# Two layers of a hybrid encoder on one core: the sixth product's own weights at byte 320 modulo 512, and the hand-over work of VectorE and ScalarE in another order

## The chip, the cores and the metric

The kernel runs on one core of a Trainium2 chip. The metric is device time of one execution in microseconds (us), lower is better. The engines are TensorE (PE in the profile; PEld its weight loads), VectorE (DVE), ScalarE (ACT), GpSimd (POOL) and SyncE (SP), which here only issues transfers. SBUF is the on-chip memory with 128 partitions, PSUM the eight banks that TensorE writes.

## The reference

Two layers over 512 tokens of width 1024, float32. Each layer:

```python
h = h + 0.5 * post(SwiGLU(pre(h)))        # w_gu: 1024 x 5632, w_down: 2816 x 1024
u = pre(h); proj = u @ w_in               # 1024 x 6912: q, k, v of three attentions, gates
m = sum_i gate_i * (branch_i @ W_branch_i)
h = h + post(m @ W_out)
h = h + 0.5 * post(SwiGLU(pre(h)))
```

`pre` and `post` are RMS norms with gains; a gate is the sigmoid of its part of `proj` plus `b_gate`. The weights of a layer are used once in a run, so they are streamed from HBM.

## The kernel before

**Split operands.** Every float32 operand of a matmul is split into a high part (rounded to float32r by a ScalarE copy) and a low part (VectorE subtracts the high part). A product is three matmuls: high by high, high by low, low by high. So each weight tile costs one ScalarE and one VectorE operation before TensorE may use it. `ensure` does this for plain streamed weights (L209, L210). Their tiles, the `r13` and `w12` below, and four tiles of the down projection (`part`, L645) share the tag `wp` with four buffers.

**The feed-forward, first half.** A few of the 22 column blocks of the gate and up weights (4, or 6 in the first) are plain products. For each of the other 16 to 18 blocks, 70 in all four feed-forwards, the 2x2 product of weight quadrants and halves of the tokens is made by seven products with sums and differences of the quadrants, in place of eight. Each is a call of `product`: twelve matmuls of 256 columns, all at L856. In a block g they stand in TensorE's queue as p1, p7, p3 of block g-1, p6, p4, p2, p5. Their weights are `h1` (p1 and p4), `h13` (p7 and p5), `h24` (p3 and p6) and their low parts, from a pool of the phase, whose tiles lie at byte 320 modulo 512; p2 alone uses `w12` (tag `wp`, at 0 modulo 512), the sixth product's own weights. Their moving operands lie at 0, but that of p5 (`t1`) at 320. p2 adds into a bank of tag `at` that ScalarE has seeded with p1's sum (L895); the others use tag `mm`. In the trace, w12 is written at L728 (ACT) and L731 (DVE), and carries the name `w`.

**The feed-forward, second half.** The down projection is seven products over 8 and one part over 6 blocks of rows, in 34 units: 4 each of kinds 1, 7, then 3 of n2, 4 of 6, 4 of 4, 3 of n1, and 4 each of 2, 5 and 3. A unit is twelve or more matmuls of 512 columns (L1096). `prep` makes the split weights of a unit (`wh` at L972 on ScalarE, `wl` at L973 on VectorE); `preps(n)` makes all up to unit n, and `then` says which load from HBM follows which preparation. `t3(c)` makes one half of the moving operand of kind 7: a difference (L1005) and its split (L999, L1000). Work beside a unit hangs on it through `job`. From the end of the blocks on, the order on TensorE, ScalarE and VectorE is that of the code (`ordered`, a manual schedule); elsewhere a scheduler places instructions.

**The hand-over.** `Handover` takes the finished sums of a sub-layer to the next operand, for four blocks of 128 tokens (`tb`): squares with their sums (L449, `junk`), the gain (L465), a root (L458), its reciprocal (L462), the addition to the residual (L474), the next norm (L487), transposes on TensorE (`turn`, L522), split copies of the transposed operand (`operand`, L531 and L532) and plain ones (`plain`, L537). `late` runs the chain for one block and calls what it is given in `between`: the first after the gain, the second between the root and the reciprocal. In a feed-forward `first_rows` does it for blocks 0 and 1 beside kind 5, and L1258 adds the last sum before kind 3 may write its bank. The function Sqrt needs a table that ScalarE loads when the first instruction asks for it (ACT_TABLE_LOAD).

**The mixer.** Three attentions, gates (tanh with half the bias, L1558) and branch products, in the order of a table; then `m @ W_out` with the hand-over beside it, in `ordered`.

Of the kernel before, what the change touches and what calls it, by code (L numbers as in the profile page):

```python
# [10 lines left out]
F32 = mybir.dt.float32  # L11
# [5 lines left out]
P = 128  # L17
# [98 lines left out]
def encoder_kernel(ctx: ExitStack, tc: tile.TileContext, order, xT, wts, cols, rows, rpb, consts, tables, out):  # L116
# [6 lines left out]
    dr = ctx.enter_context(tc.tile_pool(name="dr", bufs=1, space=bass.MemoryType.DRAM))  # L123
    phase = [None]

    BUFS = {"X": 6, "n": 2, "wr": 3, "wp": 4}
    ABUFS = {"f": {"t": 4, "x": 10}, "m": {"t": 5, "h": 4, "rr": 2, "tx": 5, "st": 16, "g": 10, "s": 2, "pt": 4}}
    PBUFS = {"mm": 4, "at": 3, "o": 1}

# [11 lines left out]
    def nm(s):  # L141
        serial[0] += 1
        return f"{s}{serial[0]}"
# [19 lines left out]
    cons = cp.tile([P, CONSTW], F32, tag="cons", name="cons")  # L163
    colt = cp.tile([P, NCOLS], F32, tag="colt", name="colt")
    ones = cp.tile([P, P], F32, tag="ones", name="ones")
    half = cp.tile([P, NCOLS], F32, tag="half", name="half")
    epst = cp.tile([P, 1], F32, tag="eps", name="eps")
    sink = cp.tile([P, L, 8], F32, tag="sink", name="sink")
    misc = cp.tile([P, 2 * L + 1], F32, tag="misc", name="misc")
# [9 lines left out]


    HB = WB // 2
    stream = {"raw": [], "ready": [], "made": 0, "held": {}, "limit": 0, "stop": NTILES * 2, "later": [], "pace": 1, "eng": nc.scalar, "beside": []}

    def wpart(name, dt=F32R):
        t = sb.tile([P, 2, HB, P], dt, tag="wp", name=nm(name), bufs=BUFS["wp"])
        return t[:, 0], t[:, 1]

    def holder(tag):
# [97 lines left out]
    def first_loads(hT):  # L286
        def load(hs, *bs):
            for b in bs:
                nc.sync.dma_start(hT[:, b, hs], xT[b * P : (b + 1) * P, hs])

        load(HALVES[0], 0)
        fetch(2, nc.sync)
        load(HALVES[0], 1, 2)
        fetch(1, nc.sync)
        load(HALVES[0], 3, 4, 5)
        fetch(1, nc.sync)
        load(HALVES[0], 6, 7)
        load(HALVES[1], *range(KD))
        nc.sync.dma_start(cons, consts)
        warm = bank("o")  # L300
        for _ in range(WARM):
            PE.matmul(warm[:, :P], ones, ones, start=True, stop=True)
        V.tensor_scalar(out=half, in0=colt, scalar1=0.5, scalar2=None, op0=ALU.mult)

    def mm3(acc, w, x, start, stop):
        if len(x[0].shape) == 3:
# [72 lines left out]
    def announce(first, spare):  # L379

        assert len(order) % HB == 0
        at = len(order) // HB
        stream["limit"] = at + len(first) * KD // HB
        held = range(at + BUFS["wp"], stream["limit"])
        stream["held"] = dict(zip(held, spare))
        assert len(held) <= len(spare)

# [17 lines left out]
    class Operand:  # L405


        def __init__(self, raw):
            form = (P, 2, KD // 2, T // 2)

            def tiles(tag, dt, name):
                return [sb.tile(list(form), dt, tag=tag, name=nm(name), bufs=BUFS[tag]) for _ in range(2)]

            self.hi, self.lo = [], []
            for _ in range(2):
                for part in (self.hi, self.lo):
                    part.append(sb.tile(list(form), F32R, tag="X", name=nm("X"), bufs=BUFS["X"]))
            self.raw = tiles("n", F32, "n") if raw else None
            h = KD // 2
            self.blocks = [(self.hi[k // h][:, :, k % h, :], self.lo[k // h][:, :, k % h, :]) for k in range(KD)]  # L420

    class Handover:

# [145 lines left out]
    def ffn(l, which, X, accs):  # L569
# [71 lines left out]
        def settle(u):  # L641

            for parts in (PH, PL):
                if u < 2:
                    t = sb.tile([P, 2, T], F32R, tag="wp", name=nm("part"), bufs=BUFS["wp"])  # L645
# [78 lines left out]
            V.tensor_tensor(out=raws[g][1][:, 1], in0=W[g]["r13"][:, 1], in1=raws[g][0][:, 0], op=ALU.add)  # L724

        def high12(g):
            W[g]["h12"], W[g]["l12"] = wpart("w12")
            A.activation(W[g]["h12"], raws[g][1][:, 0], AF.Copy)  # L728

        def low12(g):  # L730
# [351 lines left out]
        p3(count - 1)  # L1082
        silu1(count - 1)
        gated(count - 1)
        t3(1)

        a, c, e, d = [], [], [], []
# [323 lines left out]
    def mixer(l, op, first):  # L1411
# [142 lines left out]
        def gates(n, *ms):  # L1554
            for m in ms:
                pg = dense1(w, l, GL + n * KD + m, X)
                t = gate0[m // 4][:, m % 4, :] if n == 0 else big("g", name="gate")
                A.activation(t, pg, AF.Tanh, scale=0.5, bias=col("b_gate", l, n * KD + m, half))  # L1558
                gate[n, m] = t

        def combine(n, key, *ms):
# [197 lines left out]
```

## Time and profile before

| | us |
|---|---|
| median of 3 runs | 2418.13 (2414.67 to 2418.2) |
| the profiled execution | 2413.36 |
| its span | 2411.6 |
| TensorE busy | 2379.9 |
| VectorE busy | 1782.5 |
| ScalarE busy | 1342.9 |
| mean granted TensorE clock | 0.999 |

The span runs from the first to the last instruction of the profiled execution; 1.8 us of that execution lie around it. A row of the timeline gives start, length, engine, line, operation, output and inputs, shapes and, in brackets, how long the engine stood idle before it and what ended that. Ends of matmuls are modelled (0.28 us for 256 columns, 0.39 for 512) and overlap the next ones, so the pace of TensorE is read from the distances between starts. Lines of the feed-forward stand four times in a run, and those of the mixer twice.

### The profile page before, as it was taken

How to read it: one execution, taken by the hardware profiler on the slowest of the kernel's cores; microseconds unless marked ns; L12 is line 12 of the kernel's file. 1: busy time of each engine (PE TensorE's matmuls, PEld its weight loads, DVE VectorE, ACT ScalarE, POOL GpSimd, SP SyncE). 2: the span in 40 equal slices, each digit the busy share in tenths (PEclk: the TensorE clock that was granted, in tenths of full speed). 3: DMA queues.
4: the chain of work that ended last, by engine and by line, in shares of the span. 5: the costliest groups of instructions: out<-in, count | busy, mean ns of one | idle time of the engine just before them, and what ended most of it. 6: DMA issues, size and time to landing. Idle time of an engine off the chain costs nothing. (4 is left out here: it accounts for less than half of the span.)

```text
span 2411.6 us, 37743 instructions
## 1 busy us (share of the span) xinstructions
PE 2379.9 (99%) x14266; PEld 2084.2 (86%) x14266; DVE 1782.5 (74%) x2959; ACT 1342.9 (56%) x2487; POOL 193.2 (8%) x192
## 2 busy tenths in 40 slices
PE   9999999999999999999999999999999999999998
PEld 8999888888777889998899998878887778899987
DVE  8887975757667467888878878767676764788786
ACT  6555655646555365655655555556565554556563
POOL 0111000000111100110001110000011111011100
PEclk9999999999999999999999999999999999999999
DMA  5566536435443334664525565374354333246642
GB/s 172 159 169 184 172 128 179 127 105 153 118 123 97 114 105 134 170 159 164 168 89 165 159 174 192 112 184 115 115 149 124 114 96 122 97 148 168 187 144 90
DMA packets 119190, 340.46 MB, mean 141 GB/s; under 512 B 15968, under 2 KB 22752, under 8 KB 118496
## 3 DMA queue, kind: packets, MB, share of 16 engines
q1 hardware_dynamic: 91344, 224.72, 30.0%
q10 hardware_dynamic: 22032, 79.78, 11.0%
q0 software_dynamic: 5632, 33.56, 6.9%
q8 instruction: 112, 1.84, 0.3%
q14 instruction: 70, 0.57, 0.1%
HBM read 285.03 MB, written 48.23 MB: 138 GB/s over the span
## 5 line engine op out<-in xcount | busy, mean ns | idle before, releaser
L308 PE MATMUL mm<-X,w 128*128 128x512 f32 (+1 forms) x1044 | 396.0, 379 | 2.6 <-ACT w L209 1.2
L309 PE MATMUL mm<-X,w 128*128 128x512 f32 (+1 forms) x1044 | 396.4, 380 | 0.8 <-DVE X L532 0.7
L310 PE MATMUL mm<-X,w 128*128 128x512 f32 (+1 forms) x1044 | 396.1, 380 | 0.0
L210 DVE TENSOR_TENSOR w<-wr,w 128x512 fp32r<-128x512 f32 x360 | 255.1, 714 | 170.7 <-ACT w L209 168.5
L209 ACT ACTIVATE w<-wr 128x512 fp32r<-128x512 f32 x360 | 223.5, 627 | 224.7 <-PE mm L310 178.5
L856 PE MATMUL mm<-ht,l 128*128 128x256 f32 x1120 | 311.1, 278 | 0.0
L856 PE MATMUL mm<-ht,h 128*128 128x256 f32 x1120 | 311.1, 278 | 0.0
L856 PE MATMUL mm<-lt,h 128*128 128x256 f32 x1120 | 310.9, 278 | 0.0
L308 PEld LDWEIGHTS mm<-X,w 128*128 128x128 f32 x1044 | 196.8, 189 | 35.0 <-ACT X L531 1.4
L309 PEld LDWEIGHTS mm<-X,w 128*128 128x128 f32 x1044 | 196.9, 189 | 32.8 <-DVE X L532 1.1
L310 PEld LDWEIGHTS mm<-X,w 128*128 128x128 f32 x1044 | 196.6, 188 | 30.8
L856 PEld LDWEIGHTS mm<-ht,h 128*128 128x128 f32 x1120 | 210.8, 188 | 0.0
L856 PEld LDWEIGHTS mm<-ht,l 128*128 128x128 f32 x1120 | 210.8, 188 | 0.0
L856 PEld LDWEIGHTS mm<-lt,h 128*128 128x128 f32 x1120 | 210.8, 188 | 0.0
L1096 PE MATMUL mm<-wh,f 128*128 128x512 f32 x640 | 201.3, 393 | 0.0
L856 PE MATMUL mm<-X,h 128*128 128x256 f32 x1120 | 199.1, 277 | 0.0
L856 PEld LDWEIGHTS mm<-X,h 128*128 128x128 f32 x1120 | 170.1, 188 | 0.5 <-DVE v L910 0.2
L856 PE MATMUL mm<-X,l 128*128 128x256 f32 x560 | 154.9, 277 | 0.0
L1096 PEld LDWEIGHTS mm<-wh,f 128*128 128x128 f32 x640 | 120.3, 188 | 26.3
L713 DVE TENSOR_TENSOR l<-wr,h 128x1024 fp32r<-128x1024 f32 x70 | 85.7, 1224 | 70.9 <-PE mm L856 70.9
L1096 PE MATMUL mm<-wl,f 128*128 128x512 f32 x320 | 125.4, 392 | 3.1 <-DVE wl L973 3.1
L334 ACT ACTIVATE hi<-at 128x256 fp32r<-128x256 f32 (+2 forms) x168 | 73.9, 453 | 73.0 <-PE at L1389 33.6
(370 smaller groups left out, 5431.9 us busy)
## 6 DMA issues: line engine op xcount, KB each, us to landing
wr<-in_wts_dram SPq DMA_DIRECT2D x223, 512.0 KB, 4.9
wr<-in_wts_dram ACTq DMA_DIRECT2D x152, 512.0 KB, 3.7
sum<-in_wts_dram POOLq DMA_DIRECT2D x64, 512.0 KB, 5.4
st<-hi SPq DMA_DIRECT2D x84, 128.0 KB, 2.3
st<-lo SPq DMA_DIRECT2D x84, 128.0 KB, 3.2
ap<-in_wts_dram SPq DMA_DIRECT2D x20, 512.0 KB, 6.5
a<-kept SPq DMA_DIRECT2D x32, 256.0 KB, 6.2
ap<-sum SPq DMA_DIRECT2D x16, 512.0 KB, 3.3
```

The costliest lines, as they stand in the source:

```text
L209: A.activation(hi, raw, AF.Copy)
L210: V.tensor_tensor(out=lo, in0=raw, in1=f(hi), op=ALU.subtract)
L308: PE.matmul(acc, w[0], x[0], start=start, stop=False)
L309: PE.matmul(acc, w[0], x[1], start=False, stop=False)
L310: PE.matmul(acc, w[1], x[0], start=False, stop=stop)
L334: A.activation(hi, src, AF.Copy)
L713: V.tensor_tensor(out=W[g]["l1"], in0=raws[g][0], in1=f(W[g]["h1"]), op=ALU.subtract)
L856: PE.matmul(acc, ws[i], xs[j], start=start and k == n == 0, stop=stop and k == HK - 1 and n == 2, skip_group_check=True,)
L1096: PE.matmul(acc, x[i], w[j], start=start and n == 0, stop=stop and n == 2, skip_group_check=True)
```

## The change

```diff
-    BUFS = {"X": 6, "n": 2, "wr": 3, "wp": 4}
+    BUFS = {"X": 6, "n": 2, "wr": 3, "wp": 2, "wq": 2}
+    WP = BUFS["wp"] + BUFS["wq"]
+    SKEW = 80
...
-    half = cp.tile([P, NCOLS], F32, tag="half", name="half")
+    cp.tile([P, 24], F32, tag="room", name="room")
...
+    def skewed(name, at, dt=F32R):
+
+        t = sb.tile([P, 2 * T + 128], dt, tag="wq", name=nm(name), bufs=BUFS["wq"])
+        return t[:, at : at + 2 * T]
 
     def wpart(name, dt=F32R):
-        t = sb.tile([P, 2, HB, P], dt, tag="wp", name=nm(name), bufs=BUFS["wp"])
+        stream["turn"] = not stream["turn"]
+        if stream["turn"]:
+            t = sb.tile([P, 2, HB, P], dt, tag="wp", name=nm(name), bufs=BUFS["wp"])
+        else:
+            t = skewed(name, 0, dt).rearrange("p (a b c) -> p a b c", a=2, b=HB)
         return t[:, 0], t[:, 1]
...
-        V.tensor_scalar(out=half, in0=colt, scalar1=0.5, scalar2=None, op0=ALU.mult)
+        for l in range(L):
+            at = COLS["b_gate", l]
+            own = colt[:, at : at + 24]
+            V.tensor_scalar(out=own, in0=own, scalar1=0.5, scalar2=None, op0=ALU.mult)
...
+    def root_table():
+        A.activation(dummy, ones[:, 0:1], AF.Sqrt)
...
         def high12(g):
-            W[g]["h12"], W[g]["l12"] = wpart("w12")
+            t = skewed("w12", SKEW).rearrange("p (a b c) -> p a b c", a=2, b=HB)
+            W[g]["h12"], W[g]["l12"] = t[:, 0], t[:, 1]
             A.activation(W[g]["h12"], raws[g][1][:, 0], AF.Copy)
...
         p3(count - 1)
         silu1(count - 1)
         gated(count - 1)
+        preps(4)
         t3(1)
...
-        job("2", 0, move_plain)
+        job("2", 0, move_plain, root_table)
...
         region = ordered()
         region.__enter__()
         stream["eng"] = nc.sync
+        root_table()
         for k in range(KD):
...
-        H.late(1, 1, last[1], lambda: H.operand(0), lambda: weights(1))
+        H.late(1, 1, last[1], lambda: H.operand(0), lambda: None)
+        weights(1)
         H.plain(0)
```

The four buffers of tag `wp` become two of `wp` and two of `wq`; a tile of `wq` is 512 bytes longer. Streamed weights take the two kinds in turn, `r13` takes `wp` alone, `w12` takes `wq` alone and starts 80 floats, 320 bytes, into it. The down projection's `part` tiles use both kinds from their start. The tile `half` goes; the gate biases are halved in place, and a small unused tile keeps the residue modulo 512 of what lies behind it. Other tiles move by 512 bytes or by none.

Three places of the order change. At the start of a down projection, on VectorE, where `wl` are the low parts of units 2, 3 and on, and `lt` and `f` are the second half of `t3`. Before:

```order
L1000 TENSOR_TENSOR f_2817<-ht_2814,f_2816 128x1024
L924 TENSOR_TENSOR a_2520<-t_2832,v_2747 128x2x256
L1005 TENSOR_TENSOR lt_2858<-a_2520,a_1048 128x1024
L1000 TENSOR_TENSOR f_2817<-lt_2858,f_2816 128x1024
L973 TENSOR_TENSOR wl_2863<-wr_2712,wh_2862 128x1024
L973 TENSOR_TENSOR wl_2869<-wr_2765,wh_2868 128x1024
L973 TENSOR_TENSOR wl_2875<-ht_2836,wh_2874 128x1024
```

Of the change:

```order
L1022 TENSOR_TENSOR f_2818<-ht_2815,f_2817 128x1024
L946 TENSOR_TENSOR a_2521<-t_2833,v_2748 128x2x256
L995 TENSOR_TENSOR wl_2860<-wr_2713,wh_2859 128x1024
L995 TENSOR_TENSOR wl_2866<-wr_2766,wh_2865 128x1024
L1027 TENSOR_TENSOR lt_2871<-a_2521,a_1049 128x1024
L1022 TENSOR_TENSOR f_2818<-lt_2871,f_2817 128x1024
L995 TENSOR_TENSOR wl_2876<-ht_2837,wh_2875 128x1024
```

Two low parts stand ahead of the difference and its split now; ScalarE's high parts move in the same way.

Beside kinds 2 and 5 of the first feed-forward, on ScalarE, where `share` are copies of the plain part's sums and `misc` is the output of `root_table`. Before:

```order
L1154 ACTIVATE share_3440<-o_3335 128x512
L972 ACTIVATE wh_3444<-ap_3026 128x1024
L972 ACTIVATE wh_3461<-ap_3026 128x1024
L209 ACTIVATE w_3465<-wr_3275 128x512
L972 ACTIVATE wh_3480<-ap_3026 128x1024
L209 ACTIVATE w_3484<-wr_3275 128x512
L972 ACTIVATE wh_3499<-ap_3026 128x1024
L209 ACTIVATE w_3503<-wr_3311 128x512
L209 ACTIVATE w_3506<-wr_3311 128x512
L449 ACTIVATE junk_3521,sh_3522<-at_884 128x512
L196 DMA wr_3945<-in_wts_dram 128x1024
L458 ACT_TABLE_LOAD
```

Of the change:

```order
L1177 ACTIVATE share_3441<-o_3336 128x512
L438 ACT_TABLE_LOAD
L438 ACTIVATE misc<-ones 128x1
L994 ACTIVATE wh_3446<-ap_3027 128x1024
L438 ACTIVATE misc<-ones 128x1
L994 ACTIVATE wh_3463<-ap_3027 128x1024
L220 ACTIVATE w_3467<-wr_3276 128x512
L994 ACTIVATE wh_3482<-ap_3027 128x1024
L220 ACTIVATE w_3486<-wr_3276 128x512
L994 ACTIVATE wh_3501<-ap_3027 128x1024
L220 ACTIVATE w_3505<-wr_3312 128x512
```

The load stands right behind the copies. The second `misc` is the mixer's call of `root_table`: it depends on nothing, and stands in the feed-forward before the mixer. In the mixer the load stays where it was, ahead of the first root, and the number of table loads stays at 30.

In the mixer's hand-over, on VectorE, where `w` is a streamed weight's low part and `y` the normed rows of token block 1. Before:

```order
L454 TENSOR_SCALAR sh_8874<-sh_8874 128x1
L210 TENSOR_TENSOR w_8883<-wr_8818,w_8882 128x512
L462 RECIPROCAL sh_8878<-sh_8878 128x1
L487 SCALAR_TENSOR_TENSOR y_8523<-h_8519,sh_8878,gain_8529 128x512
L487 SCALAR_TENSOR_TENSOR y_8524<-h_8519,sh_8878,gain_8529 128x512
L465 TENSOR_TENSOR y_8526<-mm_8718,gain_8529 128x512
```

Of the change:

```order
L472 TENSOR_SCALAR sh_8877<-sh_8877 128x1
L480 RECIPROCAL sh_8881<-sh_8881 128x1
L505 SCALAR_TENSOR_TENSOR y_8525<-h_8521,sh_8881,gain_8531 128x512
L505 SCALAR_TENSOR_TENSOR y_8526<-h_8521,sh_8881,gain_8531 128x512
L221 TENSOR_TENSOR w_8892<-wr_8821,w_8891 128x512
L483 TENSOR_TENSOR y_8528<-mm_8721,gain_8531 128x512
```

The low part stands behind the two norms now. TensorE's order and those of GpSimd and SP are unchanged.

More of the change, by code (lines that the diff above doesn't have):

```diff
@@ L181, in encoder_kernel @@
     HB = WB // 2
-    stream = {"raw": [], "ready": [], "made": 0, "held": {}, "limit": 0, "stop": NTILES * 2, "later": [], "pace": 1, "eng": nc.scalar, "beside": []}
+    stream = {"raw": [], "ready": [], "made": 0, "held": {}, "limit": 0, "stop": NTILES * 2, "later": [], "pace": 1, "eng": nc.scalar, "beside": [], "turn": False}
+    def skewed(name, at, dt=F32R):
+        t = sb.tile([P, 2 * T + 128], dt, tag="wq", name=nm(name), bufs=BUFS["wq"])
+        return t[:, at : at + 2 * T]
     def wpart(name, dt=F32R):
-        t = sb.tile([P, 2, HB, P], dt, tag="wp", name=nm(name), bufs=BUFS["wp"])
+        stream["turn"] = not stream["turn"]
[3 more added lines that the diff above has]
+            t = skewed(name, 0, dt).rearrange("p (a b c) -> p a b c", a=2, b=HB)
         return t[:, 0], t[:, 1]
@@ L383, in announce @@
         stream["limit"] = at + len(first) * KD // HB
-        held = range(at + BUFS["wp"], stream["limit"])
+        held = range(at + WP, stream["limit"])
         stream["held"] = dict(zip(held, spare))
@@ L644, in settle @@
                 if u < 2:
-                    t = sb.tile([P, 2, T], F32R, tag="wp", name=nm("part"), bufs=BUFS["wp"])
+                    if u == 0:
+                        t = sb.tile([P, 2, T], F32R, tag="wp", name=nm("part"), bufs=BUFS["wp"])
+                    else:
+                        t = skewed("part", 0).rearrange("p (a b) -> p a b", a=2)
                     parts.append([t[:, 0, :], t[:, 1, :]])
@@ L1557, in gates @@
                 t = gate0[m // 4][:, m % 4, :] if n == 0 else big("g", name="gate")
-                A.activation(t, pg, AF.Tanh, scale=0.5, bias=col("b_gate", l, n * KD + m, half))
+                A.activation(t, pg, AF.Tanh, scale=0.5, bias=col("b_gate", l, n * KD + m))
                 gate[n, m] = t
```

## The prediction

> **What bounds the kernel now.** I read the shares of the engines first, then the windows inside a feed-forward stage, then who waited for whom on TensorE.
>
> ```profile
> PE 2379.9 (99%) x14266; PEld 2084.2 (86%) x14266; DVE 1782.5 (74%) x2959; ACT 1342.9 (56%) x2487; POOL 193.2 (8%) x192
> ...
> 2190.00:2199.69 9.69, 9.69 (x87) 9.69 (x86) 1.00 0.69 166
> ...
> PE mm L1096 <- DVE ht L1258: 3.5, 3, 1.2
> PE mm L1096 <- DVE wl L973: 3.1, 4, 0.8
> ...
> PE at L522 <- DVE y L487: 1.7, 2, 0.8
> ...
> PE mm L308 <- ACT X L531: 0.6, 2, 0.3
> ```
>
> TensorE is busy for 99% of the span. The window (its length, then PE and PEld busy, granted clock, DMA share, GB/s) is one block of a feed-forward's gate and up weights: 9.69 us without a hole at clock 1.00. So only two things shorten the run: matmuls that issue closer together, and the few stalls in the last four rows (total, times, longest, in us). The change touches both.
>
> **Part A: the sixth product's weights.** The `product` calls of a block run on TensorE as p1, p7, p3 (of the block before), p6, p4, p2, p5, twelve matmuls of 256 columns each.
>
> ```profile
> L856 PE MATMUL at<-X,w 128*128 128x256 f32 x840 | 111.9, 283 | 0.0
> ...
> 2218.90 0.28 PE L856 MATMUL mm<-ht,h 128*128 128x256 f32 x1
> ...
> 2220.33 0.40 PE L856 MATMUL mm<-X,h 128*128 128x256 f32 x2
> ...
> 2227.15 1.60 PE L856 MATMUL at<-X,w 128*128 128x256 f32 x12
> 2228.58 0.28 PE L856 MATMUL mm<-ht,h 128*128 128x256 f32 x1
> ```
>
> Only p2 writes an `at` bank, so the first row is p2: 840 matmuls, 70 blocks. In one block p5 runs from 2218.90 to 2220.33 (1.43 us), then p1, p7, p3, p6 and p4 to 2227.15 (6.82 us, 1.364 each), then p2 to 2228.58 (1.43). Two products take 0.066 us more than the other five, with the same shapes. What sets these two apart is where their operands lie modulo 512 bytes, in the program's placement: p2 has weights and moving operand both at 0, p5 both at 320; the other five have weights at 320 and moving operands at 0. The change puts p2's weights at 320. Of all matmuls in the program, these 840 alone change their pair of residues.
>
> The other side is bounded by the opening products of a stage, also 256 wide:
>
> ```profile
> 12.24 0.28 PE L308 MATMUL mm<-X,w 128*128 128x256 f32 x1
> ...
> 13.67 0.28 PE L308 MATMUL at<-X,ht 128*128 128x256 f32 x1
> ...
> 16.50 0.28 PE L308 MATMUL mm<-X,w 128*128 128x256 f32 x1
> ```
>
> Twelve with both operands at 0 take 1.43 us (119 ns each); 24 with weights at 320 (`ht`, `lt`) take 2.83 us (118 ns). There the residue buys 1 ns; these change bank every three matmuls, p2 stays in one. If p2 behaved like them, 840 x 1 ns = 0.8 us would come. No row shows a residue pair of this kind that loses. I take p2 as nearest to p4, same line, same shape and one bank: 70 x 0.066 = **4.6 us**, ends 0.8 and 5.0.
>
> The Trainium skill, "TensorE: Matmul & The Clock Gate", section "Step-by-step: what each phase is for", says that TensorE has two independent SBUF read ports, so that loading the next weights takes no read bandwidth from the running matmul. By that rule the place of the weights would not matter and part A would be 0. The 1.43 against 1.364 us above speaks against it here.
>
> p2's tile comes from a pool of two now, where w12 could take any of four buffers. ScalarE's write of block g+1's w12 so waits for p2 of block g-1:
>
> ```profile
> 2219.76 0.64 ACT L728 ACTIVATE w<-wr 128x512 fp32r<-128x512 f32 x1 [0.27 <-DMA wr<-in_wts_dram]
> ...
> 2222.74 0.36 ACT L895 ACTIVATE at<-mm 128x256 f32<-128x256 f32 x1
> ```
>
> p2 of g-1 ended by 2218.90, 0.86 us before that write. Behind it on ScalarE stands the seed copy (L895), which p2 of block g needs at 2227.15, 4.05 us after the copy's end at 2223.10. Cost: nothing.
>
> **Part B: two preparations ahead of `t3(1)`.** Four feed-forwards, the start of the down projection, all alike; the first:
>
> ```profile
> 231.87 0.33 SPq L950 DMA_DIRECT2D wr<-in_wts_dram  x1
> ...
> 237.69 0.68 DVE L924 TENSOR_TENSOR a<-t,v 128x512 f32<-128x512 f32 x1
> 238.41 1.23 DVE L1005 TENSOR_TENSOR lt<-a,a 128x1024 f32<-128x1024 f32 x1
> 240.76 1.23 DVE L1000 TENSOR_TENSOR f<-lt,f 128x1024 fp32r<-128x1024 f32 x1 [1.13 <-ACT f L999]
> 241.90 2.35 DVE L973 TENSOR_TENSOR wl<-wr,wh 128x1024 fp32r<-128x1024 f32 x2
> ...
> 239.67 1.06 ACT L999 ACTIVATE f<-lt 128x1024 fp32r<-128x1024 f32 x1 [2.68 <-DVE lt L1005]
> ...
> 241.77 0.62 PE L1096 MATMUL mm<-wh,f 128*128 128x512 f32 x2
> 243.18 0.50 PE L1096 MATMUL mm<-wl,f 128*128 128x512 f32 x1 [0.78 <-DVE wl L973]
> ```
>
> TensorE wants the third unit's low part at 241.77 plus two steps of 0.23, 242.23, and gets it at 243.18: 0.95 us lost. Now both `wl` stand right behind `a<-t,v`, which ends at 238.37, and their ScalarE halves run in the 2.68 us in which ScalarE idled. The first `wl` is ready near 239.6, so the stall goes. What is late next: `f<-lt` moves behind two 1.2 us operations, to some 244.2; TensorE wants it for the third unit of product 7, six units of 2.75 us after 236.4, near 253. The fourth unit's load, issued at 231.87, now holds both engines if it is late; it has 6 us until then, against a median landing time of 4.9 us for such loads. 4 x 0.95 = **3.8 us**, ends 0 and 3.8.
>
> **Part C: the square-root table early.** In the three feed-forwards that hand over to a next stage (first one shown):
>
> ```profile
> 317.09 1.06 ACT L972 ACTIVATE wh<-ap 128x1024 fp32r<-128x1024 f32 x1 [1.26 <-PE at L1096]
> ...
> 325.99 1.28 ACT L458 ACT_TABLE_LOAD   x1
> ...
> 327.49 0.58 ACT L449 ACTIVATE junk<-at 128x512 f32<-128x512 f32 x1
> ...
> 326.74 0.68 DVE L465 TENSOR_TENSOR ap<-at,ht 128x512 f32<-128x512 f32 x1
> 328.19 0.69 DVE L465 TENSOR_TENSOR ap<-at,ht 128x512 f32<-128x512 f32 x1 [0.77 <-ACT junk L449]
> 328.80 0.15 DVE L462 RECIPROCAL sh<-sh 128x1 f32<-128x1 f32 x1
> ...
> 338.61 0.47 PE L1096 MATMUL mm<-wh,f3x 128*128 128x512 f32 x1 [1.23 <-DVE ht L1258]
> ...
> 2389.10 0.69 DVE L1258 TENSOR_TENSOR ht<-mm,ht 128x512 f32<-128x512 f32 x1 [2.01 <-PE mm L1096]
> ```
>
> The load of 1.28 us stands between the two squares, the second square holds VectorE's second `ap`, and VectorE then works through one chain to L1258, for which TensorE waits 1.23 us. With the load gone from there the second square ends near 326.8, before the first `ap` does, so the second `ap` follows at once, at 327.35: 0.84 us earlier, and so L1258. Of the 1.23 us some 0.4 stay. The load moves to ScalarE behind the `share` copies, where the next operations waited 1.26 us for TensorE; the small activation with it and the mixer's, which the order shows in the same place in two feed-forwards, fit there too. In the last feed-forward L1258 waited 2.01 us for TensorE itself: no gain. The mixer's own call moves no load (below). 3 x 0.84 = **2.5 us**, ends 0 and 3.7 (all three stalls of 1.23).
>
> **Part D: the mixer's hand-over**, two of them:
>
> ```profile
> 865.57 0.29 ACT L458 ACTIVATE sh<-sh,sh 128x1 f32<-128x1 f32 x1
> ...
> 867.25 0.60 ACT L449 ACTIVATE junk<-mm 128x512 f32<-128x512 f32 x1
> ...
> 866.42 0.69 DVE L210 TENSOR_TENSOR w<-wr,w 128x512 fp32r<-128x512 f32 x1 [1.35 <-ACT w L209]
> ...
> 867.22 1.42 DVE L487 SCALAR_TENSOR_TENSOR y<-h,sh,gain 128x512 f32<-128x512 f32 x2
> 868.55 0.68 DVE L465 TENSOR_TENSOR y<-mm,gain 128x512 f32<-128x512 f32 x1
> ...
> 868.03 0.66 PE L522 MATMUL at<-cons,y 128*128 128x128 f32 x4 [0.84 <-DVE y L487]
> ...
> 871.75 0.58 ACT L531 ACTIVATE X<-at 128x512 fp32r<-128x512 f32 x1
> ```
>
> VectorE waits 1.35 us at `w`, and the two `y` behind it hold TensorE's transposes. With `w` behind them they start at 866.1, right after the root (865.57 + 0.29), and that wait of TensorE goes. But the chain to the `X` copy at 871.75, for which TensorE waits next, gains less: `w` still runs before `y<-mm`, which moves from 868.55 to 868.04, 0.51 us. TensorE arrives earlier and waits longer there. Net 2 x 0.51 = **1.0 us**, ends 0 and 1.7 (both waits of the transposes).
>
> The halved gate biases (two operations of 24 columns in place of one of 146) run in the opening, where VectorE is not what TensorE waits for; cost nothing.
>
> **Sum.** 4.6 + 3.8 + 2.5 + 1.0 = 11.9 us. The profiled execution took 2413.4 us (span 2411.6 and 1.8 around it), so 2401.5 by its own scale; that run lies 4.8 us under the median of 2418.1. Against the median: **2406.2 us**.
>
> **Rivals.** (1) The place of the weights does not matter, or works as in the opening (0.8): 2418.1 - 7.3 = 2410.8 for no gain at all. Against it: p2 and p5 are slow, and their five siblings of the same shape are not. (The first half of this rival is what the rule of the Trainium skill under part A comes to.) (2) The hand-over stalls are replaced by equal ones on the same chains (C and D zero): 2418.1 - 8.4 = 2409.7. For it: in D a second wait stands 4 us behind the first. (3) The edits do less than they say. The mixer's early table is of this kind: in the order its small activation stands in the feed-forward before, and the load stays where it was. If (1) and (2) both hold, or B fails with one of them, 3.5 to 4.6 us stay: 2414. (4) Slower: the two-buffer pool. If the release of w12's buffer came later than the 4.05 us of slack behind L728, p2 would wait for its seed in all 70 blocks. Each 0.1 us past it costs 7 us; from 0.17 us on the change loses, and at 0.3 us it gives 2406.2 + 21 = 2427. Against it: the buffer's last reader ends 0.86 us before the write starts.
>
> **Chances.** Forecast 0.70; (1) 0.10; (2) 0.07; (3) 0.09; (4) 0.04. A measurement of this kernel can tell about 0.2% (4.8 us) from no change. The forecast, (1) and (2) are faster by more: 0.87; (3) is the same: 0.09; slower 0.04. The range reaches from all four parts at their best ends (5.0 + 3.8 + 3.7 + 1.7 = 14.2, 2403.9) less the 3.5 us by which one of the shown runs lies under the median, 2400.5, to (1) with some scatter, 2413.
>
> **What would show it.** A: twelve `at<-X,w` of L856 take 1.37 us, a block 9.62. B: no TensorE wait for `wl` L973 at the four starts. C: the wait for L1258 near 0.4 us, the table load right behind `share`. D: no wait for `y` L487 and a longer one for `X` L531. I am wrong if p2 still takes 1.43 us, or if a new wait of TensorE on ScalarE appears in the blocks.

## The result, and the profile after

| | us |
|---|---|
| median of the changed kernel, 4 runs | 2402.09 (2401.48 to 2404.16) |
| median of the kernel before, 4 runs beside them | 2417.06 (2414.67 to 2418.2) |
| ratio, with its 95% interval | 0.9942 (0.993 to 0.9954) |
| profiled execution after, its span | 2402.65, 2400.9 |

The change is 15.0 us faster by the medians and 10.7 us by the two profiled executions. First the page of the changed kernel, its shares and the group of p2, the counterparts of rows of the prediction:

```profile
PE 2373.5 (99%) x14266; PEld 2080.6 (87%) x14266; DVE 1780.8 (74%) x2960; ACT 1342.4 (56%) x2493; POOL 192.7 (8%) x192
...
L878 PE MATMUL at<-X,w 128*128 128x256 f32 x840 | 106.9, 276 | 0.0
```

And TensorE's waits (total, times, longest):

```profile
PE mm L322 <- ACT X L549: 1.7, 2, 0.9
...
PE mm L1119 <- DVE ht L1281: 1.0, 3, 0.4
```

The 840 matmuls of the sixth product take 106.9 us as a group, against 111.9. The wait for `wl` (3.1 in four) is no longer in the list, nor the transposes' wait for `y`; the wait for the sum of v22 is down from 3.5 to 1.0 us, and the one for `X` up from 0.6 to 1.7.

The pace of TensorE is read best as a count of matmuls in a window of fixed length without a hole. The window view of the kernel before, and then of the changed one; the columns are as in the prediction, and the first two windows lie in the blocks and in the down projection of the second feed-forward, the third in the down projection of the last:

```profile
960.00:1060.00 100.00, 100.00 (x870) 100.00 (x870) 82.99 (x105) 58.29 (x95) 16.47 (x20) 1.00 0.60 161
1115.00:1165.00 50.00, 50.00 (x220) 41.05 (x219) 44.66 (x44) 25.24 (x28) 0.00 (x0) 1.00 0.63 210
```

```profile
960.00:1060.00 100.00, 100.00 (x878) 100.00 (x877) 84.70 (x107) 59.05 (x95) 18.23 (x22) 1.00 0.61 163
1115.00:1165.00 50.00, 50.00 (x220) 41.01 (x219) 41.23 (x40) 22.97 (x24) 0.00 (x0) 1.00 0.62 210
2320.00:2370.00 50.00, 50.00 (x220) 41.05 (x219) 40.75 (x45) 29.46 (x39) 0.00 (x0) 1.00 0.42 137
```

The two kernels issue 870 against 878 matmuls in 100 us of the blocks, and both 220 in 50 us of the down projection, at clock 1.00.

The start of the first down projection after the change, VectorE:

```profile
237.36 0.69 DVE L946 TENSOR_TENSOR a<-t,v 128x512 f32<-128x512 f32 x1
237.97 2.35 DVE L995 TENSOR_TENSOR wl<-wr,wh 128x1024 fp32r<-128x1024 f32 x2
240.24 1.22 DVE L1027 TENSOR_TENSOR lt<-a,a 128x1024 f32<-128x1024 f32 x1
242.58 1.23 DVE L1022 TENSOR_TENSOR f<-lt,f 128x1024 fp32r<-128x1024 f32 x1 [1.12 <-ACT f L1021]
```

Both `wl` stand behind `a<-t,v` and end at 240.3, before TensorE wants the third unit (its start is 236.0 and two units of 2.75 later, 241.5). And the hand-over, ScalarE in the first feed-forward, with what TensorE still waits for there and in the mixer:

```profile
312.76 0.58 ACT L1177 ACTIVATE share<-o 128x512 f32<-128x512 f32 x1
313.37 1.28 ACT L438 ACT_TABLE_LOAD   x1
...
323.82 0.58 ACT L467 ACTIVATE junk<-at 128x512 f32<-128x512 f32 x1
...
336.26 0.47 PE L1119 MATMUL mm<-wh,f3x 128*128 128x512 f32 x1 [0.41 <-DVE ht L1281]
...
871.01 0.38 PE L322 MATMUL mm<-X,w 128*128 128x256 f32 x1 [0.88 <-ACT X L549]
```

The load now stands behind the `share` copies, 10 us ahead of the squares.

### The profile page after: what moved, and what is told of

Same layout as the page of the kernel before. It is cut to its first block, busy times and chain, and to the rows that moved or that the text cites. A ratio compares the mean times of both kernels' runs of the same rounds, so it can differ in the third digit from the quotient of the medians.

```text
span 2400.9 us, 37750 instructions
## 1 busy us (share of the span) xinstructions
PE 2373.5 (99%) x14266; PEld 2080.6 (87%) x14266; DVE 1780.8 (74%) x2960; ACT 1342.4 (56%) x2493; POOL 192.7 (8%) x192
## 5 line engine op out<-in xcount | busy, mean ns | idle before, releaser
L1119 PEld LDWEIGHTS mm<-wh,f 128*128 128x128 f32 x640 | 120.2, 188 | 25.5
```

What stands on the lines that cost most here:

```text
L1119: PE.matmul(acc, x[i], w[j], start=start and n == 0, stop=stop and n == 2, skip_group_check=True)
```

## Experiments

All kernels here issue the same matmuls in the same order on TensorE. So two traces can be laid over each other matmul by matmul, and the distance from each start to the next subtracted. "Pace" below is the mean of such distances; where the text gives a pace of a product or of 48 matmuls in a row, it is worked out from the trace in this way. This table gives the differences to the profiled execution of the kernel before, in us, one execution each:

| kernel | p2 | other products of the blocks | waits at the start of the down projection | pace in the down projection | hand-over of the feed-forward | all else | sum |
|---|---|---|---|---|---|---|---|
| before, once more | 0 | -0.4 | 0 | 0 | +0.1 | +2.1 | +1.8 |
| changed kernel | -5.0 | -0.9 | -3.8 | -0.9 | -2.4 | +2.3 | -10.7 |
| place alone (e1) | -5.0 | -1.2 | 0 | +2.0 | +0.2 | +3.5 | -0.5 |
| order alone (e2) | 0 | -0.3 | -3.8 | +5.5 | -3.9 | +1.9 | -0.6 |
| places swept (e4) | -1.8 | -0.6 | -3.8 | -0.9 | -2.8 | +3.3 | -6.6 |
| preparations alone (e5) | 0 | -0.3 | -3.8 | +5.5 | -0.8 | +1.7 | +2.4 |
| table alone (e6) | 0 | -0.1 | 0 | 0 | -2.1 | +3.3 | +1.0 |
| place and preparations (e8) | -5.0 | -1.2 | -3.8 | -0.9 | +0.5 | +4.6 | -5.8 |
| fifth product moved (e9) | -1.6 | +14.8 | -3.8 | +5.5 | -3.6 | +2.2 | +13.5 |
| three places (e13) | -3.8 | -0.3 | -3.8 | -0.9 | -2.7 | +1.8 | -9.7 |
| waits left (e14) | -5.0 | -1.0 | -3.8 | -1.2 | -4.5 | +5.1 | -10.4 |
| what worked (e15) | -5.1 | -6.1 | -3.8 | -1.2 | -4.0 | +1.9 | -18.2 |
| matched tile (e16) | 0 | -0.3 | -3.8 | +0.9 | +0.4 | +0.5 | -2.3 |

"All else" holds the opening, the attentions and the mixers, the change's part there with it. The kernel before differs from itself by 2.1 there, so what a kernel gains in all is read from the medians, and where it gains from the columns in the middle. The 2.1 come from the opening: in the repeated execution TensorE waited 2.53 us there for a weight tile, against 1.19, and 15 of the matmuls behind that wait came every 213 ns. Equal windows behind the wait, of the first execution and of the repeated one:

```profile
10.90:14.30 3.40, 3.40 (x30) 3.40 (x30) 3.40 (x8) 3.40 (x9) 0.00 (x0) 1.00 0.93 330
```

```profile
11.70:15.10 3.40, 3.40 (x18) 3.40 (x19) 2.41 (x5) 2.18 (x6) 0.00 (x0) 0.54 0.83 264
```

The granted clock (the column ahead of the DMA share) was 0.54 over this window, and 0.50 over the 2.8 us from 12.1 on. A stretch of 14 or 15 such matmuls, which costs some 1.4 us, stands in the opening of eight of the fourteen traces (the changed kernel, e3, e4, e8, e9, e13, e14 and e15), and not in that of the profiled execution before. So the sums of the table set these eight against a trace without it.

**e1, the place alone**: the changed kernel with its three moves of work undone (`preps(4)`, both calls of `root_table`, the mixer's `weights(1)`).

> The change with its three edits of the order undone: only p2's weights at byte 320 modulo 512, with the two kinds of buffers. Theory (the residue pair sets p2's pace): twelve at<-X,w matmuls of p2 take 1.37 us in place of 1.43, 70 blocks give 4.6 to 5.6 us, ratio to before near 0.998. The stalls at wl (0.8 us four times), at the last sum before kind 3 (1.2 us three times) and at the mixer's y (0.8 us twice) stay. Rival (the order does it all): p2 takes 1.37 us but the run is no faster, or p2 stays at 1.43.

Measured: 2409.86 us (2406.82 to 2412.85), before 2416.39; 0.9971 (0.996 to 0.9983). p2 gains 5.0 us, as in the whole change. But the down projection of the last feed-forward lost 2 us. The window view of this kernel:

```profile
960.00:1060.00 100.00, 100.00 (x878) 100.00 (x877) 83.98 (x105) 58.45 (x96) 17.29 (x21) 1.00 0.60 161
1115.00:1165.00 50.00, 50.00 (x220) 41.09 (x219) 43.13 (x42) 24.30 (x26) 0.00 (x0) 1.00 0.60 205
2320.00:2370.00 50.00, 50.00 (x216) 40.54 (x216) 40.34 (x44) 25.37 (x31) 0.00 (x0) 1.00 0.40 131
```

216 matmuls of 512 columns in 50 us, where the others have 220: 233.3 ns each in place of 228.9, at the same granted clock and without a hole. This stage has two paces, and here the wait for `wl`, from which the slow one starts, began it.

**e2, the order alone**: the changed kernel with `SKEW = 0`.

> The whole change with SKEW = 0: p2's weights back at byte 0 modulo 512, same buffers, same order as the change. Theory: p2 takes 1.43 us again, the stalls go as in the change, 3.8 + 2.5 + 0.8 = 7.1 us by the sum of stalls, ratio near 0.997. With the run of the skew alone it adds up to the change. Rival (the change's 15 us between the medians against 10.7 between the two profiles is a gain that neither part explains): the two runs together stay under 11 us.

Measured: 2412.78 (2411.18 to 2415.4), 0.9985 (0.9977 to 0.9994). The waits went (-3.8, and -3.9 in the hand-over), but the down projections ran at 233.3 ns nearly throughout, which cost 5.5. Part of the 3.9 is TensorE, slower here, coming later to the same sum: e5, with the hand-over of the kernel before, gains 0.8 there.

**e3, the kernel before once more**, for the scatter of one execution.

> The kernel before once more, for its own scatter: which stalls repeat and which do not. Theory: the stalls at wl, at the last sum and at the mixer's y come back within 0.1 us each, while the waits in the attention stages (each 0.3 to 1.8 us) come back changed by some us in sum, as they did between the two profiles of before and after, where they took back 1.9 us. Rival: the attention waits repeat as well, and the 1.9 us are the change's doing.

2415.19. The waits for `wl`, for v22 and for `y` came again within 0.1 us. In both traces of this kernel the first 24 matmuls of each down projection go at 233.4 ns, up to the wait for `wl`, and those behind it at 228.9. How the stage comes to be entered slow is seen at the end of the blocks, where p5, p2 and p3 stand in this order: p4 runs at 113.3 ns, p3, behind p2 with both operands at 0, at 118, in all four feed-forwards of both traces (and of e2 and e5). Inside the blocks p5, with both at 320, stands behind p2, and the products behind p5 run at 113.3, all but the first few matmuls of p1.

**e4, w12 of block g at byte 32 x (g modulo 16)**: every place in one run.

```diff
+    SWEEP = [8 * n for n in range(16)]
-            t = skewed("w12", SKEW).rearrange("p (a b c) -> p a b c", a=2, b=HB)
+            t = skewed("w12", SWEEP[g % len(SWEEP)]).rearrange("p (a b c) -> p a b c", a=2, b=HB)
```

> The change, with w12 of block g at byte 32 x (g modulo 16) of its buffer, in place of 320 for all: the pace of p2 by the residue of its weights, its moving operand at 0. Theory (equal residues cost): twelve take 1.43 us at 0 only and 1.36 to 1.37 at all others, or at 32 and 480 something between. Rival (a graded clash by distance): the pace falls from 120 ns to 113.6 over several steps of 32 bytes and 320 is not special. Rival (two independent reads, the place does not matter and something else in the buffers did it): all 16 the same.

Measured: 2406.73. p2's pace in ns by its weights' place (moving operand at 0, at least 48 matmuls at each place); the second row is for 256 bytes more:

| byte | 0 | 32 | 64 | 96 | 128 | 160 | 192 | 224 |
|---|---|---|---|---|---|---|---|---|
| ns | 119.8 | 118.4 | 113.3 | 120.3 | 118.2 | 119.2 | 113.3 | 116.3 |
| ns, 256 on | 119.7 | 118.9 | 113.3 | 120.2 | 117.9 | 119.2 | 113.3 | 116.5 |

The place repeats every 256 bytes, and 64 and 192 are the quick ones (320 is 64 past 256). Without the last blocks, in which p2 stands behind p5, 32 gives 118.9 in both rows and 224 gives 116.3. Except in block 0, p2 was entered at the quick pace here. The Trainium skill, "TensorE: Matmul & The Clock Gate", section "Step-by-step: what each phase is for", has two independent read ports and loads of weights that take nothing from the running matmul. Here the place of the weights alone moves a matmul of 256 columns between 113.3 and 120.3 ns, and the measurement decides.

**e5, the preparations alone**: e2 with the table and the mixer undone too; only `preps(4)` ahead of `t3(1)` is left.

> The changed kernel with the sixth product's weights back at byte 0 modulo 512 and the parts on the root table and the mixer undone: the two preparations ahead of t3(1) alone. Theory I (the sum of independent parts): the four waits of TensorE for the third unit's low part go, 4 x 0.95 = 3.8 us, and nothing else changes: 0.9984 of the kernel before. Theory II (TensorE's pace in the down projection is carried over from the slow sixth product until a stall breaks it): the four waits go as well, but with them what ended the slow pace. The down projection's 512-wide matmuls, at 233.4 ns up to the wait and 228.9 ns behind it in the kernel before, then stay near 233.3 ns over most of the stage in most feed-forwards, which cost 5.5 us in the run of the order without the place; the sum is then +1.7 us, 1.0007, and under no account below 0.999.

Measured: 2416.06 (2413.82 to 2418.8), before 2416.08; 1.0001 (0.9992 to 1.001). Window view:

```profile
1115.00:1165.00 50.00, 50.00 (x216) 40.49 (x215) 44.28 (x43) 26.18 (x29) 0.00 (x0) 1.00 0.61 207
2320.00:2370.00 50.00, 50.00 (x216) 40.49 (x215) 39.56 (x41) 25.30 (x31) 0.00 (x0) 1.00 0.41 135
```

The waits went, 3.8 us, and the pace took 5.5 back: the wait for `wl` had been what ended the slow pace. The sum of independent parts (0.9984) lies outside the interval; the interaction was foreseen at 1.0007.

**e6, the early table of the feed-forward alone.**

> The kernel before with only the early root table of the feed-forward's hand-over. Three waits of TensorE for the sum of v22 shrink from 1.2 to 0.4 us, 2.5 us less, 0.9990 of the kernel before; the wait for the third unit's low part (0.95, four times) and the first chunk of the down projection (231.3 ns) stay as before. If the load's going were worth nothing, the wait would stay at 1.2 or another of 0.8 would stand within 10 us behind it.

2413.43 (2410.7 to 2415.68), 0.9987 (0.9978 to 0.9996): 2.6 us by the medians, as expected, and 2.1 in the hand-over of its trace. The waits of this kernel, where the sum of v22 stands at L1280:

```profile
PE mm L1118 <- DVE wl L995: 3.1, 4, 0.8
...
PE mm L1118 <- DVE ht L1280: 1.4, 3, 0.6
```

**e8, place and preparations together** (table and mixer undone).

> The changed kernel with the parts on the root table and the mixer undone: place and preparations together. Theory I: 5.0 + 0.6 + 3.8 = 9.4 us less, 0.9961. Theory II: the down projection is entered at the quick pace, and no wait breaks it: 228.9 ns from its first matmul to the stage's end in all four feed-forwards, 0.9 us more, so 10.3 us less, 0.9957. The two differ little in time; the pace by chunks of 48 matmuls tells them apart, 231.3 against 228.9 in the first chunk, and no chunk at 233.3 as the place alone had in its last feed-forward.

2404.79 (2403.82 to 2407.6), 0.9952 (0.9939 to 0.9966). The down projection is entered at 228.9 ns in all four feed-forwards and keeps it. So the preparations, worth nothing alone, are worth 4 to 5 us on top of the place (0.9971 to 0.9952).

**e9, the fifth product's `t1` at byte 0**: the changed kernel with the gaps around `t1` removed or moved, so that p5's operands lie at 320 and 0 as those of the other six (48 matmuls of an opening come to 0 with it).

```diff
-            gap("gap1", 80)
             between = lambda: operand(1)
...
             accs = begin(X.blocks, firsts_of(l, 0), ("mm", "at"), (), between)
+            gap("gap1", 80)
...
-                some(at(gap, "gap1", 80), at(divide, "t1"), at(gap, "gap2", 48)) if not first else at(divide, "t1"),
+                at(divide, "t1"),
```

> The changed kernel with t1, the fifth product's moving operand, moved from byte 320 to byte 0 modulo 512; its weights stay at 320. If what counts is how the two operands of a matmul stand to each other (weights 64 or 192 modulo 256 bytes past the moving operand were the quick places in the run that swept the sixth product's weights, 0 a slow one), p5's 840 matmuls go from 118.5 to 113.6 ns: 4.1 us less than the changed kernel, near 2398.0, 0.9926 of the kernel before at 2416.4. If only the weights' own place counted (320 good, 0 bad), p5 would have been quick already; if only p2 has this property, p5 stays at 118.5 and the time at 2402.

Measured: 2425.99 (2424.12 to 2427.4), 1.004 (1.0027 to 1.0053): slower than either kernel, where 4 us less were expected. Window view:

```profile
960.00:1060.00 100.00, 100.00 (x851) 100.00 (x851) 82.72 (x104) 58.32 (x94) 16.45 (x20) 1.00 0.58 159
1115.00:1165.00 50.00, 50.00 (x216) 40.51 (x215) 44.58 (x45) 28.06 (x32) 0.00 (x0) 1.00 0.52 174
```

851 in 100 us. All seven products run at 117.8 ns from the first block to the last, and the down projection is entered at 233.4. The matmuls of the blocks that ran at 113.3 ns in the changed kernel have their operands at the same addresses modulo 512 here; what is gone is the product with equal residues among them. In the changed kernel block 0 starts at 117.8 too, and the pace turns to 113.3 with the third matmul behind the first p5. So 113.3 belongs to no place alone: at the same places there is a slow and a quick pace, each keeps itself up, and something in the stream has to throw TensorE from one into the other.

**e13, three other places for w12 in the kernel of e9**: byte 0 in block 0, 96 in block 5, 224 in block 10.

```diff
-            t = skewed("w12", SKEW).rearrange("p (a b c) -> p a b c", a=2, b=HB)
+            t = skewed("w12", {0: 0, 5: 24, 10: 56}.get(g, SKEW)).rearrange("p (a b c) -> p a b c", a=2, b=HB)
```

> The kernel of e9_fifth (t1 at byte 0, so that no product of a block has its two operands at one residue), with the sixth product's weights at byte 0 in block 0, at 96 in block 5 and at 224 in block 10 of each feed-forward, at 320 in all others. In e9_fifth all seven products ran at 117.8 ns from the first block to the last, in the changed kernel at 117.8 only until block 0's fifth product, whose operands both lie at 320, and at 113.3 from then on. Theory (two paces that keep themselves up, and a product with equal residues throws TensorE from the slow one into the quick one): one of the three products, likeliest the one in block 0, does that too; the products behind it run at 113.3 to the stage's end, p5 among them: some 4 us less than the changed kernel, near 2398 if block 0 does it. Rival (p5's equal residues act on the products near them only, or an unequal p5 is slow in itself): every product of all blocks stays at 117.8 as in e9_fifth, 2426.

Measured: 2403.69. In each of the four feed-forwards the pace stayed at 117.8 behind the place 0 of block 0, went from 117.8 to 113.3 with the place 96 of block 5, p5 among the quick ones, and stayed there past the place 224 of block 10. Window view, ahead of block 5 and behind it in the second feed-forward:

```profile
935.00:955.00 20.00, 20.00 (x172) 20.00 (x171) 16.13 (x21) 11.30 (x19) 3.31 (x5) 1.00 0.54 161
985.00:1005.00 20.00, 20.00 (x179) 20.00 (x179) 17.41 (x23) 11.63 (x21) 3.57 (x4) 1.00 0.71 169
```

Two paces are shown by this. That equal residues as such throw TensorE into the quick one is refuted: p2 with both operands at 0 leaves it slow here, and in the kernel before turned quick into slow at the end of the blocks; p5 with both at 320 makes it quick, and so did 96 against 0.

**e14, what the changed kernel left of its waits**: three edits to it.

```diff
-        upto = {7: 11, 8: 12, 9: 13, 10: 14, 26: 30, 27: 30, 28: 30, 29: 32, 30: 32}
+        upto = {7: 11, 8: 12, 9: 13, 10: 14, 26: 30, 27: 30, 28: 30, 29: 31, 30: 31}
...
-                        t = skewed("part", 0).rearrange("p (a b) -> p a b", a=2)
+                        t = skewed("part", SKEW).rearrange("p (a b) -> p a b", a=2)
...
         H.late(0, 1, last[0], lambda: weights(1), lambda: None)
-        weights(1)
...
         H.late(1, 1, last[1], lambda: H.operand(0), lambda: None)
-        weights(1)
+        weights(2)
```

> The changed kernel with what it left of its waits taken on: unit 31's preparation behind add22_(0) in place of ahead of it, and one of the mixer's weights(1) moved from behind late(0) to behind late(1). And the parts of the n1 and n2 units' second tile at byte 320, where the preparations they are multiplied with lie. If the 0.5 us left at L1281 are VectorE's preparation ahead of it, they go in three feed-forwards, 1.4 us; if they are the chain behind the two squares, they stay. If the wait for X in the mixer (0.9 and 0.8) comes from VectorE's w ahead of the second gain, it falls to 0.4 and 0.3, 1.0 us; else it stays. The 192 matmuls of the second tile go from 228.9 to 226.7 ns as the third tile's in the first feed-forward, 0.4 us. All three: 2399.3, 0.9930 of the kernel before at 2416.2; none: 2402.1, 0.9942.

Measured: 2402.95 (2401.08 to 2403.8), 0.9939 (0.9925 to 0.9952): no better than the changed kernel. Two of the edits worked: the wait at L1281 went in all three feed-forwards (0.66, 0.57 and 0.46 us), and the second tile's matmuls went at 226.7 to 227.5 ns, 0.35 us in all. The third went the wrong way. VectorE in the first mixer of the changed kernel, and then VectorE and TensorE in that of this one:

```profile
866.58 0.68 DVE L221 TENSOR_TENSOR w<-wr,w 128x512 fp32r<-128x512 f32 x1
867.18 0.68 DVE L483 TENSOR_TENSOR y<-mm,gain 128x512 f32<-128x512 f32 x1
```

```profile
866.36 1.29 DVE L221 TENSOR_TENSOR w<-wr,w 128x512 fp32r<-128x512 f32 x2
867.57 0.69 DVE L483 TENSOR_TENSOR y<-mm,gain 128x512 f32<-128x512 f32 x1
...
871.39 0.38 PE L322 MATMUL mm<-X,w 128*128 128x256 f32 x1 [1.48 <-ACT X L549]
```

The gain that TensorE's `X` hangs on is the third, `late(2)`, and I had put a second `w` ahead of that one: 0.6 us more, in both mixers. It names the cause of what part D left: `w` ahead of the third gain. The hole had a price of its own in the first mixer, read in the window view behind it and behind the same hole of the second:

```profile
871.30:875.60 4.30, 3.86 (x17) 3.67 (x18) 4.16 (x9) 2.60 (x7) 0.00 (x0) 0.60 0.19 71
2059.50:2063.80 4.30, 3.76 (x30) 3.57 (x31) 4.06 (x8) 2.69 (x7) 0.00 (x0) 1.00 0.19 75
```

The granted clock was 0.60 over the 4.3 us behind the first hole, 0.50 from 872.6 to 875.2, where 14 matmuls of 256 columns came every 213 ns; behind the second hole it was 1.00.

**e15, what worked, together**: e9's `t1` at 0; w12 at byte 96 in block 0 alone; e14's first two edits; and in the mixer

```diff
-            t = skewed("w12", SKEW).rearrange("p (a b c) -> p a b c", a=2, b=HB)
+            t = skewed("w12", 24 if g == 0 else SKEW).rearrange("p (a b c) -> p a b c", a=2, b=HB)
...
         H.late(1, 1, last[1], lambda: H.operand(0), lambda: None)
-        weights(1)
         H.plain(0)
-        weights(1)
...
-        H.late(2, 1, last[2], lambda: weights(1), lambda: H.operand(1))
+        H.late(2, 1, last[2], lambda: None, lambda: H.operand(1))
+        weights(2)
```

> The changed kernel with what the runs so far point to: t1 at byte 0; the sixth product's weights at byte 96 in block 0 alone, which threw TensorE into the quick pace in block 5 of the run with three such places; the second tile of parts at byte 320; unit 31's preparation behind add22_(0); and the mixer's weights(1) that stood ahead of the third gain moved behind late(2), since the run before showed that this one, and not that behind late(0), lies on the chain to X. Expected against the changed kernel's 2402.1: p5 840 x 5 ns = 4.2 us, blocks 1 to 15 or 17 otherwise as there; 1.7 from add22_(0); 0.35 from the parts; 1.0 from the wait for X (0.9 to 0.4, twice). 2394.9, 0.991 of the kernel before. If the byte 96 works in block 5 only, all products stay at 117.8 and the time is near 2423; if the wait for X stays, 1.0 more.

Measured: 2393.97 us (2393.71 to 2395.31), 0.9909 (0.9896 to 0.9923) of the kernel before at 2416.07: faster than both. Windows of this kernel, and its wait for `X`:

```profile
960.00:1060.00 100.00, 100.00 (x885) 100.00 (x884) 85.51 (x108) 60.06 (x97) 18.25 (x22) 1.00 0.62 165
1115.00:1165.00 50.00, 50.00 (x221) 41.09 (x220) 40.72 (x41) 23.99 (x29) 0.00 (x0) 1.00 0.58 200
```

```profile
PE mm L322 <- ACT X L549: 0.6, 2, 0.3
```

There are 885 matmuls in 100 us now, and the wait for `X` is back at 0.3 each. In the first mixer 0.5 us of this gain went again: the transposes after that start 0.3 and 0.2 us later than before.

**e16, a matched tile in the down projection of e5**: `part`'s second tile at byte 320, sixth product's weights at 0. In the down projection the split weights `wh` and `wl`, 512 columns wide, are the moving operand and lie at 320, and `f` and `part`, 128 columns wide, are the operand that is loaded; so `t3`, which the part on the kernel before has making the moving operand, makes the loaded one.

> The two preparations ahead of t3(1) alone (as e5_preps_only, sixth product's weights at byte 0), and the second tile of parts at byte 320, equal to its moving operand's. In e5_preps_only the down projection ran at 233.3 ns to its end in the second to fourth feed-forward, and in the first up to the third n2 unit, the only one there whose two operands have one residue. If such a unit ends the slow pace, it now ends at the second n2 unit in all four: chunks one and two at 233.3, from the fourth on 228.9, some 1.4 us less in each of three feed-forwards than e5_preps_only. If the first feed-forward's change had another cause, the second to fourth stay at 233.3 throughout.

Measured: 2411.14. Window view behind that tile in the second feed-forward, of this kernel and then of e5:

```profile
1130.00:1160.00 30.00, 30.00 (x133) 24.61 (x132) 27.51 (x29) 17.99 (x19) 0.00 (x0) 1.00 0.64 214
```

```profile
1130.00:1160.00 30.00, 30.00 (x130) 24.30 (x129) 26.90 (x27) 17.75 (x19) 0.00 (x0) 1.00 0.57 193
```

There are 133 against 130 matmuls in 30 us. In all four feed-forwards the first 120 matmuls of the stage go at 233.3 ns, and those behind the tile at 228.9; in e5 the second to fourth stayed at 233.3 to the end. So the down projection's slow pace can be thrown off by one tile.

## Why the prediction was right, and where it was not

The forecast of 2406.2 lay 4.1 us above the median measured, 2402.09, which is inside the range and on the side that was named.

- **Part A, 4.6 us: the size was right (5.0), the reason only half.** p2 lost its slow pace, and e4 shows that the weights' place does it. But the prediction made the pace a property of a product's own place ("what sets these two apart is where their operands lie"), and took p4 as the measure for it. e9 shows p4, with nothing changed about its operands, at 117.8. The quick pace of the five siblings was upheld by the stream around them; p2 at its new place joined it. Had p5 lain at 0 as well, the same edit would have been part of a kernel at 2426: that p5 lay where it did was luck. "No row shows a residue pair of this kind that loses" was true of that trace, and no reason to expect that none does.
- The opening's 118 ns, which the prediction put down to the change of bank every three matmuls, need no such cause: the products of e9 stay in one bank and run at 117.8.
- **Part B, 3.8 us: the waits went to the hundredth (3.8), the term stood only by the company of A.** Alone it is worth nothing (e5). The step that failed is the sum, which set B beside A as independent, and it came out by luck: p2 at byte 0 hands a slow pace to the down projection, and the wait for `wl` was what ended it; without the wait the stage keeps it, 5.5 us. With A the stage is entered at the quick pace, and 0.9 us come on top, which no term held: 0.4 in the first 24 matmuls of the four stages, and the rest in the matmul behind each wait, 342 ns long before and some 230 now.
- **Part C, 2.5 us: right.** 0.8 to 0.9 us in each of three feed-forwards, and 0.2 to 0.4 left where 0.4 were forecast; e6 shows it alone, and e14 that the rest was `wl` of unit 31 ahead of L1281.
- **Part D, 1.0 us: right** (2.2 less at the transposes, 1.2 more at `X`). The cause given, `w` still ahead of a gain, was right too; e14 made it worse by a second `w` and e15 took it away.
- **The sum.** The four parts measured 5.0 + 3.8 + 2.5 + 1.0 = 12.3 in the traces against 11.9; unforeseen were 0.9 in the other products and 0.9 in the pace of the down projection. The medians differ by 15.0, the two traces by 10.7: the profiled execution of before was quick in the opening, where the repeated one was 2.1 slower by a longer wait and the 15 matmuls at half clock behind it; the trace of the changed kernel has such a stretch too. Whether other executions of the kernel before also hold stretches at half clock, or at the slow pace, which would help to explain why they spread over 7 us (17 runs beside e1, 2413.0 to 2420.4) and those of the changed kernel and of e15 over 2.7 and 1.6 (only 4 and 5 runs, which spread less in any case), was not traced and stays open.
- **The rivals.** That the place doesn't matter fell with e1 and e4. That the hand-over's waits are replaced by equal ones held for half of the transposes' wait in D only, as forecast. The mixer's own early call moved no table load, as said: its load stands at 852.6 us under the hand-over's root, before at 853.4. The slower rival, a buffer that comes free late, did not occur: the group of p2 shows 0.0 us of idle.

## What to carry to other kernels

A product that is slower than its siblings by a few per cent at full clock and without a hole is a reason to count matmuls in windows for each stage, and to try where its weights lie modulo 256 bytes against the moving operand; but judge the whole stage, not the product, since the pace of matmuls is handed on from one to the next. A stall can be worth less than its length where it resets such a pace, so an edit that removes one belongs in a run by itself and in one with the other edits. When a wait moves, follow the chain to the very instruction that TensorE waits for before moving work off it: two neighbours of the same line can stand on different chains.

## What the runs showed of the hardware that was not expected

- Two paces, at granted clock 1.00 and with the operands at the same places: 113.3 and 117.8 ns for 256 columns, 228.9 and 233.3 for 512, some 4.4 ns per matmul in both. Each lasts: all 490 products of e9 went at 117.8. Products with operands at other places switch it: p5 with both at 320 made it quick in all four feed-forwards of the changed kernel, and 96 against 0 in all four of e13 and of e15; both at 0 left or made it slow in all four of e13 and of the kernel before; 224 against 0 left it quick in all four of e13. In the down projection a tile with both at 320 made it quick in 4 of 4 (e16). A hole did both: the wait for `wl` ended the slow pace in the eight cases of the two traces of before, and began it in the last feed-forward of e1. Shorter ones did too: in the first feed-forward of the profiled execution before, the pace of block 0 turns quick behind one distance of 174 ns, and that of block 1 slow behind two of 280 and 222; in the changed kernel two of 264 and 221 at the same matmuls left it quick. Why these and not others stays open.
- Matmuls of 512 columns want the opposite of those of 256: with equal residues they take 226.7 ns and with 64 apart modulo 256 at best 228.9, where 256 columns take 118 to 120 with equal ones and 113.3 apart. The plain products of 512 columns, with both operands at 0, agree: the median distance of those that write `at` is 227 ns in the kernel before. One place was not tried: in all fourteen traces the 192 matmuls of `m @ W_out` with the moving weights at 0 and the loaded operand at 320 go at 233.2 ns, and those of the same product with both at 320 at a median of 227. Worked out from these, the former at 320 might save 192 x 6 ns = 1.2 us, an estimate.
- A hole of 1.48 us and one of 0.34 behind it brought the granted clock to 0.50 for some 3 us in one mixer of e14 and left it at 1.00 in the other. In the openings a wait of 1.5 to 2.5 us did so in eight traces, and one of 1.2 to 2.2 us did not in six (before, e1, e2, e5, e6 and e16): the length of the hole alone does not tell. The Trainium skill, "TensorE: Matmul & The Clock Gate", section "What's actually happening", has the clock fall to half after an idle window of about 3.4 us that runs freely. The granted 0.50 agrees with a half, but the holes here were shorter than that window.
